# First feed-forward operands made ahead and kept in DRAM, and the step to the feed-forward without GpSimd arithmetic

## The chip, the cores and the metric

The kernel runs on one core of a Trainium2 chip. The metric is the device time of one execution in microseconds; a comparison takes the median of several executions. One execution was also recorded by the hardware profiler, and that one is read below.

## The reference

One encoder block on a sequence of 1024 tokens with 1024 channels, all float32. The part that matters here is the border between its two sub-layers:

```python
y = mixed @ w_out[l]
x = layer_norm(ALPHA * x + g1[:, None, :] * y, ln1_g[l], ln1_b[l])

h = modulate(layer_norm(x), sh2, sc2)
gt, up = jnp.split(h @ w_ffn_in[l], 2, axis=-1)          # 1024 x 2*2816
y = (jax.nn.silu(gt) * up) @ w_ffn_out[l]
x = layer_norm(ALPHA * x + g2[:, None, :] * y, ln2_g[l], ln2_b[l])
```

## The kernel before

**Number format.** Every float32 operand of a matrix product is kept as two float32r halves: `hi`, a cast on ScalarE, and `lo`, the difference source minus `hi`. The helper `split` (L96, L97) makes the pair, the difference on VectorE or on the engine it is given. A product is then three matmuls, hi·hi, hi·lo and lo·hi (`mm3`, L100 to L102).

**Stages.** Eight attention heads run one after the other, each in eight steps j; projections for the next head and other small jobs are put between the scores. Then come the eight token tiles of the output projection (`y0` to `y7`, 48 matmuls of 128x512 each), their residual, two layer norms and modulation, and a transpose by PE back to channels-by-tokens. Then the feed-forward runs over 22 column blocks f of 128, gate and up together, and its second matrix follows.

**The feed-forward as seven products.** Gate and up halves against the two token halves are multiplied by the Strassen-Winograd scheme: seven block products in place of eight. With token tiles 0 to 3 as the first half (`b11`, `b21`: upper and lower channels, in `h0h` and `h0l`) and tiles 4 to 7 as the second half (x12 and x22, in the raw tile `hr`), the activation side needs these operands, each with a hi and a lo:

- t1 = x12 − b11 (in `o1`), t2 = x22 − t1, in `oA`
- t3 = t2 − b11 in effect, also in `oA`; it is the same as x22 − x12
- b22 = x22 and t4 = b21 − t2, both in `oB`.

The weight side needs, for each f, the plain gate blocks (r11, r12: `first_w`, products `first_mm` into the PSUM tiles `fa` and `fb`), and five more operands: s1 = r21 + r22, s2 = s1 − r11, s3 = r11 − r21, s4 = r12 − s2 and r22 itself. For f = 0 the five are made by `rest_w` (L958 on) in six parts; for later f by the loop of the feed-forward. For f below 4 the plain products are made in the step itself and kept in the `p1` tiles.

**The step** is the stretch between the output projection and the feed-forward loop. It stands in a block with a manual schedule: on PE, VectorE, ScalarE and GpSimd the instructions stand exactly in the order in which they are written; each engine works its list in that order and waits at each instruction for what it needs. In the heads the order on each engine is made by a scheduler from priorities.

The short names of the step, with token tile t: `R` residual, `S1`/`A` statistics and affine of the first norm, `S2`/`N` the same of the second (`N`, L472, writes the normalised tile), `T` the transposes on PE, `M` the modulation on ScalarE (eight activations), `H` the split of tiles 0 to 3, `X` x12 − b11 (two subtractions, L1024 and L1025), `X2` t2 and `X2h`/`X2l` its halves, `X3` t3 and t4 in five parts, `B22h`/`B22l` the halves of b22, and `first_cp`/`first_add` the evacuation of a `first_mm`. `rstd` (L437, L93) are two tiny GpSimd instructions on which `A` and `N` wait. GpSimd also makes the lo of the four first weights (`wg_l`, 128x1024), the lo of b22, two of three steps of t3, one of t4 and two sums of `rest_w`.

At the end of f = 0 the products come in this order: a·t2, c·t1 (both in `rest_a`), a·t3, c·b22, a·t4, where a and c are the PSUM tiles `fa0` and `fc0`. ScalarE copies a (`u2`) and c (`p5`) after the first two, and VectorE adds a to `p5` (L1293) before a·t4 may write a again.

Of the kernel before, what the change touches and what calls it, by code (L numbers as in the profile page):

```python
# [35 lines left out]
def encoder_block_kernel(  # L36
# [445 lines left out]
    with ExitStack() as ctx2:  # L482
# [230 lines left out]


# [94 lines left out]
        for h in range(NH):  # L809
# [18 lines left out]
            else:  # L828
# [27 lines left out]
            for j in range(8):  # L856
# [56 lines left out]
    def first_w(f, rawg, eng=None):  # L913
# [44 lines left out]
    def rest_w(f, rawg, rawu, step):  # L958

        r11, r12, r21, r22 = rawg[:, 0:4, :], rawg[:, 4:8, :], rawu[:, 0:4, :], rawu[:, 4:8, :]  # L960
        if step == 0:
            ops_[f] = []
            ops_[f, "s"] = [evp.tile([P, 4, P], F32, tag="st", bufs=2, name="ws%d_%d" % (f, i)) for i in range(2)]

        def op_split(src):
            n = len(ops_[f])
            o = (fp.tile([P, 4, P], F32R, tag="oh", bufs=4, name="oh%d_%d" % (f, n)),
                 fp.tile([P, 4, P], F32R, tag="ol", bufs=4, name="ol%d_%d" % (f, n)))
            split(*o, src)
            ops_[f].append(o)  # L970

        sa, sb = ops_[f, "s"]
        if step == 0:
            pol(sa, r21, r22, op=ALU.add)
        elif step == 1:
            vec(sb, sa, r11, op=ALU.subtract)
            op_split(sb)
        elif step == 2:
            op_split(sa)
            pol(sa, r11, r21, op=ALU.subtract)  # L980
            vec(sb, r12, sb, op=ALU.subtract)
        elif step == 3:
            op_split(sa)
        elif step == 4:
            op_split(sb)
        else:
            op_split(r22)

    def X3(t, step):
        o11, o21 = [[o.bitcast(F32) for o in cut(b, t)] for b in (b11, b21)]  # L990
        x = hr[:, 4:8, tcol(t)]
        e = pol if t < 7 else vec
        if step == 0:
            f4_[t] = (ev_tile if t < 6 else th_tile)("h4s%d" % t).rearrange("p (a b) -> p a b", b=P)
            vec(f4_[t], o21[0], tt2[t], op=ALU.subtract)
        elif step == 1:
            e(x, tt2[t], o11[0], op=ALU.subtract)
            e(x, x, o11[1], op=ALU.subtract)
        elif step == 2:
            split(*cut(t3, t), x)  # L1000
        elif step == 3:
            pol(f4_[t], f4_[t], o21[1], op=ALU.add)
        else:
            split(*cut(t4, t), f4_[t])
# [60 lines left out]
    with tc.manual_schedule(engines={nc.vector.engine, nc.gpsimd.engine, nc.tensor.engine, nc.scalar.engine}):  # L1065
# [4 lines left out]
        R(5); S1(5); H(2); A(5); S2(5); N(5); H(3)  # L1070
        T(4); M(4)
# [20 lines left out]
        cps.close()
# [481 lines left out]
```

## Time and profile before

| | |
|---|---|
| median of 3 runs | 1627.44 us (1627.05 to 1629.0) |
| the profiled execution | 1627.82 us, span of its instructions 1626.0 us |
| mean granted TensorE clock | 0.986 |
| PE busy | 1564.6 us (96% of the span) |
| VectorE busy | 1170.9 us (72%) |
| ScalarE busy | 705.2 us (43%) |
| GpSimd busy | 359.1 us (22%) |

The span is read from the start of the first instruction. The heads end at about 845 us, the output projection runs to about 953 us, the step and f = 0 to about 1016 us, the feed-forward to about 1400 us. A busy PE is not a PE at its peak; what counts is where it is idle and at which clock it works.

### The profile page before, as it was taken

Reading aid. Unit: us, or ns where it says so; the run is one execution under the profiler, and the core shown is the slowest. Engines: PE = TensorE matmul, PEld = TensorE weight load, DVE = VectorE, ACT = ScalarE, POOL = GpSimd, SP = SyncE. Lnnn points to the kernel's source line nnn. Section 1 sums busy time; section 2 is a strip of 40 time slices with the busy share of each in tenths; the row PEclk is TensorE's granted clock in tenths of the full one; section 3 lists DMA queues with packets and bytes.
Section 4 is the critical chain, followed back from the end, with each engine's and each line's share of the span. In section 5 each row is a group of like instructions: output and inputs, shape, how many; then the busy total and the mean of one; then the engine's idle time right before and its main releaser. Section 6 shows DMA issues by size and latency. Waiting matters only on the chain. (4 is left out here: it accounts for less than half of the span.)

```text
span 1626.0 us, 20759 instructions
## 1 busy us (share of the span) xinstructions
PE 1564.6 (96%) x7634; PEld 1305.5 (80%) x7634; DVE 1170.9 (72%) x1690; ACT 705.2 (43%) x1224; POOL 359.1 (22%) x361
## 2 busy tenths in 40 slices
PE   5899999999999999999999986999999999999996
PEld 3787888888888888888878864888888888888885
DVE  7675868597775767576575799877877888436488
ACT  3445445454454545454471343444444444323220
POOL 4300001010001211100052255434333344100013
PEclk9999999999999999999999998999999999999999
DMA  9244415142332433221326631766666665996673
GB/s 333 59 114 143 139 62 147 59 136 88 109 102 71 150 110 92 78 52 47 91 97 203 192 117 38 240 229 211 233 233 223 230 227 182 349 398 228 201 269 133
DMA packets 187001, 260.79 MB, mean 160 GB/s; under 512 B 9682, under 2 KB 127507, under 8 KB 186899
## 3 DMA queue, kind: packets, MB, share of 16 engines
q1 hardware_dynamic: 181488, 244.75, 45.7%
q0 software_dynamic: 2448, 9.44, 1.5%
q10 hardware_dynamic: 2962, 5.27, 0.9%
q8 instruction: 60, 0.98, 0.2%
q14 instruction: 43, 0.34, 0.1%
HBM read 173.97 MB, written 77.07 MB: 154 GB/s over the span
## 5 line engine op out<-in xcount | busy, mean ns | idle before, releaser
L638 ACT ACTIVATE e<-e,nm 128x1024 f32<-128x1024 f32 x128 | 147.1, 1150 | 112.3 <-DVE nm L636 111.0
L636 DVE CUSTOM_DVE_ANT_0 e<-s,table 128x1024 f32<-128x1024 f32 x128 | 153.1, 1218 | 23.5 <-PE s L631 23.1
L97 DVE TENSOR_TENSOR al<-at,ah 128x512 fp32r<-128x512 f32 x128 | 83.2, 684 | 32.1 <-ACT ah L96 31.5
L629 PE MATMUL s<-k,q 128*128 128x512 f32 x256 | 105.2, 411 | 1.2 <-DVE nm L636 1.2
L631 PE MATMUL s<-k,q 128*128 128x512 f32 x256 | 101.5, 397 | 0.0
L96 ACT CAST oh<-ws 128x512 fp32r<-128x512 f32 x88 | 54.0, 616 | 85.7 <-POOL ws L1296 44.9
L97 DVE TENSOR_TENSOR ol<-ws,oh 128x512 fp32r<-128x512 f32 x88 | 73.5, 835 | 21.1 <-ACT oh L96 21.1
L643 DVE SCALAR_TENSOR_TENSOR e<-e,c,e 128x1024 f32<-128x1024 f32 x64 | 87.0, 1359 | 1.9
L97 DVE TENSOR_TENSOR fw<-fw,fw 128x512 fp32r<-128x512 f32 x77 | 82.1, 1066 | 0.2 <-ACT fw L96 0.2
L96 ACT CAST ah<-at 128x512 fp32r<-128x512 f32 x128 | 70.2, 597 | 27.7 <-PE at L652 27.6
L1296 POOL TENSOR_TENSOR ws<-rg,ru 128x512 f32<-128x512 f32 x21 | 44.3, 2110 | 148.3 <-DVE ol L97 140.7
L652 PE MATMUL at<-ident,e 128*128 128x128 f32 x512 | 69.8, 277 | 5.3 <-DVE e L643 3.2
L100 PE MATMUL av<-ah,vh 128*128 128x256 f32 x256 | 73.8, 288 | 0.3 <-ACT ah L96 0.2
L102 PE MATMUL av<-ah,vl 128*128 128x256 f32 x256 | 72.5, 283 | 0.0
L101 PE MATMUL av<-al,vh 128*128 128x256 f32 x256 | 72.4, 283 | 0.0
L100 PE MATMUL fa<-oA,oh 128*128 128x512 f32 x176 | 69.4, 395 | 2.7 <-ACT oh L96 2.7
L101 PE MATMUL fa<-oA,oh 128*128 128x512 f32 x176 | 69.4, 395 | 0.8 <-DVE oA L1052 0.8
L102 PE MATMUL oa<-w,mol 128*128 128x512 f32 x176 | 68.6, 390 | 1.2 <-DVE mol L97 1.2
L102 PE MATMUL fa<-oA,ol 128*128 128x512 f32 x176 | 69.3, 394 | 0.0
L100 PE MATMUL oa<-w,moh 128*128 128x512 f32 x176 | 68.6, 390 | 0.0
L101 PE MATMUL oa<-w,moh 128*128 128x512 f32 x176 | 68.5, 389 | 0.0
L652 PEld LDWEIGHTS at<-ident,e 128*128 128x128 f32 x512 | 59.4, 145 | 11.0 <-DVE e L643 3.6
(573 smaller groups left out, 4636.7 us busy)
## 6 DMA issues: line engine op xcount, KB each, us to landing
wfD<-fw SPq DMA_DIRECT2D x77, 512.0 KB, 3.4
w<-wfD SPq DMA_DIRECT2D x77, 512.0 KB, 4.8
ada<-in_w_ada_dram SPq DMA_DIRECT2D x32, 512.0 KB, 3.9
rg<-in_w_ffn_in_dram SPq DMA_DIRECT2D x26, 512.0 KB, 4.0
ru<-in_w_ffn_in_dram SPq DMA_DIRECT2D x22, 512.0 KB, 3.9
fw<-in_w_ffn_out_dram SPq DMA_DIRECT2D x44, 256.0 KB, 4.4
midD<-th SPq DMA_DIRECT2D x42, 256.0 KB, 2.2
q<-q SPq DMA_DIRECT2D x32, 256.0 KB, 2.9
```

The costliest lines, as they stand in the source:

```text
L96: nc.scalar.copy(hi, src)
L97: (eng or nc.vector).tensor_tensor(lo, src, hi.bitcast(F32), op=ALU.subtract)
L100: nc.tensor.matmul(ps, lh, rh, start=start, stop=False, skip_group_check=skip)
L101: nc.tensor.matmul(ps, lh, rl, start=False, stop=False, skip_group_check=skip)
L102: nc.tensor.matmul(ps, ll, rh, start=False, stop=stop, skip_group_check=skip)
L629: nc.tensor.matmul(ps[:, cs], q[:, 0, jj * P:(jj + 1) * P], kd[h, m][:, cs], start=True, stop=False)
L631: nc.tensor.matmul(ps[:, cs], q[:, 1, jj * P:(jj + 1) * P], kd[h, m][:, cs], start=False, stop=True)
L636: nc.vector.tensor_tensor_reduce(out=t, in0=ps, in1=table[:, o0:o0 + S], scale=-slope, scalar=3.0e38, op0=ALU.add, op1=ALU.min, accum_out=nm)
L638: nc.scalar.activation(t, t, AF.Exp, bias=nm, scale=-1.0, accum_out=zt[:, m, j:j + 1])
L643: nc.vector.scalar_tensor_tensor(s[1], s[1], c1, s[0], op0=ALU.mult, op1=ALU.add)
L652: nc.tensor.matmul(pt[:, i, :], a[:, kt * P:(kt + 1) * P], ident, start=True, stop=True, is_transpose=True)
L1296: pol(sa, blocks(n)[0], blocks(n)[2], op=ALU.subtract)
```

## The change

There are two parts.

**Weights ahead.** In heads 6 and 7 a generator, `ffn_units`, is called once for each step j from the second step of head 6 on. Each call makes one split of a 128x512 weight block into the tile `acc` (hi on ScalarE, lo on VectorE) and stores the pair to DRAM by SP's queue: eight units for the plain gate blocks of f = 1, 2, 3 and 0 (`wgD`), five for the operands of f = 0 (`opD`), thirteen in all, with four GpSimd additions in place and five loads of 512 KB. In the step, `first_w` and `first_op` load the finished halves by GpSimd's own DMA queue: eight loads of 512 KB and ten of 256 KB.

**The step.** `rest_w` is gone. t3 is now made as x22 − x12 (`D3`, `D3h`, `D3l`) before x12 is overwritten by `X`; the lo of b22 and both steps of t4 are on VectorE; the order of the parts is another. `early(1)`, the output tile 1, moves from the tail of head 7 to its last step.

```diff
+    wgD = dram.tile([4, 2, P, 2, HF], F32, tag="wgD", name="wgD")
+    opD = dram.tile([5, 2, P, HF], F32, tag="opD", name="opD")
...
+        def ffn_units():
...
+            def unit(dst, src, nm):
+                t = at.tile([P, 2, HF], F32R, tag="acc", name=nm)
+                split(t[:, 0, :], t[:, 1, :], src)
+                nc.sync.dma_start(dst.rearrange("a p c -> p a c"), t.bitcast(F32))
...
+            for f in (1, 2, 3):
+                yield from halves_of(f, gcols(f))
+            rg, ru = gcols(0), load_raw(wcols(wfi, DFF), "eu0")
+            yield from halves_of(0, rg)
+            r11, r12, r21, r22 = block(rg, 0), block(rg, 1), block(ru, 0), block(ru, 1)
+            unit(opD[4], r22, "ou4")
+            yield
+            pol(r22, r21, r22, op=ALU.add)
+            unit(opD[1], r22, "ou1")
...
-                    7: [lambda: rms_mix(h, 0, 1), lambda: early(0)],
+                    7: [lambda: rms_mix(h, 0, 1), lambda: early(0), lambda: early(1)],
...
+                elif h >= 6 and (h, j) > (6, 0):
+                    next(units, None)
...
-        split(*w, rawg, eng)
+        for a in range(2):
+            nc.gpsimd.dma_start(w[a].rearrange("p a b -> p (a b)").bitcast(F32),
+                                wgD[f, a].rearrange("p h c -> p (h c)"))
...
+    def first_op(n):
...
+        for a in range(2):
+            nc.gpsimd.dma_start(o[a].rearrange("p a b -> p (a b)").bitcast(F32), opD[n, a])
...
+    def D3(t):
+        d3_[t] = evp.tile([P, 4, P], F32, tag="st", bufs=2, name="d3_%d" % t)
+        vec(d3_[t], hr[:, 4:8, tcol(t)], hr[:, 0:4, tcol(t)], op=ALU.subtract)
...
+    def X3(t):
...
+        vec(f4_[t], o21[0], tt2[t], op=ALU.subtract)
+        vec(f4_[t], f4_[t], o21[1], op=ALU.add)
...
-        pol(o[1], hr[:, 4:8, tcol(t)], o[0].bitcast(F32), op=ALU.subtract)
+        vec(o[1], hr[:, 4:8, tcol(t)], o[0].bitcast(F32), op=ALU.subtract)
...
-        w_[0] = first_w(0, gload(0), nc.gpsimd)
         out_mm(6, mt[6], y_[6], (1,))
         T(5); M(5)
-        R(6); S1(6); X(4); A(6); S2(6); X(5); N(6)
-        w_[1] = first_w(1, gload(1), nc.gpsimd)
+        R(6); S1(6); D3(4); X(4); A(6); S2(6); D3(5); N(6); X(5)
+        w_[1] = first_w(1)
...
+        M(6); B22h(4); D3h(4); B22h(5); D3h(5)
+        R(7); S1(7); B22l(4); X2(4); A(7); S2(7)
         first_mm(0, w_[0])
         first_cp(0)
...
+        X2h(4)
         first_mm(1, w_[1])
+        first_add(0, False); N(7); T(7)
...
+        M(7)
+        w_[2] = first_w(2)
...
+        first_mm(2, w_[2])
+        w_[3] = first_w(3)
+        first_op(0)
+        D3(7); X(7); X2(7)
+        X2h(7); D3h(6); B22h(7); D3h(7)
+        first_cp(2)
...
+        X3s(4); X3(6); X3s(5); X3(7); X3s(6); X3s(7)
```

**Where the order moves.** GpSimd in the step, from the tiny `rstd` of token tile 7 on; before, with `wg_l` the lo of a first weight, `ws` a sum of `rest_w`, `oB` b22, `hr` t3:

```order
L437 TENSOR_SCALAR m_7rs<-m_7mv 128x1
L93 TENSOR_TENSOR m_7rs<-m_7rs,mhalf 128x1
L97 TENSOR_TENSOR wg_l<-rg_8456,wg_h 128x1024
L97 TENSOR_TENSOR wg_l<-rg_8503,wg_h 128x1024
L974 TENSOR_TENSOR ws_0_8543<-ru_8541 128x512
L1040 TENSOR_TENSOR oB<-hr,oB 128x4x128
L997 TENSOR_TENSOR hr<-hr,h0h 128x4x128
L998 TENSOR_TENSOR hr<-hr,h0l 128x4x128
L997 TENSOR_TENSOR hr<-hr,h0h 128x4x128
L998 TENSOR_TENSOR hr<-hr,h0l 128x4x128
L980 TENSOR_TENSOR ws_0_8543<-rg_8539,ru_8541 128x512
L997 TENSOR_TENSOR hr<-hr,h0h 128x4x128
```

and now, with `oh` and `ol` the halves of an operand of f = 0:

```order
L439 TENSOR_SCALAR m_7rs<-m_7mv 128x1
L95 TENSOR_TENSOR m_7rs<-m_7rs,mhalf 128x1
L964 DMA wg_h<-wgD 128x1024
L964 DMA wg_l<-wgD 128x1024
L964 DMA wg_h<-wgD 128x1024
L964 DMA wg_l<-wgD 128x1024
L973 DMA oh_0_8629<-opD 128x512
L973 DMA ol_0_8630<-opD 128x512
L973 DMA oh_1_8646<-opD 128x512
L973 DMA ol_1_8647<-opD 128x512
```

Arithmetic on GpSimd between these points is gone, and DMA issues stand there, behind the `rstd` of tile 7.

ScalarE at the end of f = 0, before; `p_3` is the copy of `fa3`, `u_0` and `p_0` the copies of a and c, `oB` the hi of t4, `th_0` the tanh of the gate, `oh` hi of weight operands:

```order
L929 COPY p_3_8654<-fa_8610 128x512
L1059 COPY u_0_8669<-fa_8415 128x512
L1062 COPY p_0_8683<-fc_8656 128x512
L96 CAST oh_3_8686<-ws_1_8544 128x512
L96 CAST oB<-h4s_8531 128x4x128
L96 CAST oB<-h4s_8533 128x4x128
L96 CAST oB<-h4s_8535 128x4x128
L96 CAST oB<-h4s_8648 128x4x128
L96 CAST oh_4_8698<-ru_8541 128x512
L1240 ACTIVATE th_0_8712<-p_0_8441 128x512
```

and now:

```order
L986 COPY p_3_8692<-fa_8663 128x512
L1090 COPY u_0_8717<-fa_8492 128x512
L1093 COPY p_0_8731<-fc_8704 128x512
L98 CAST oB<-h4s_8698 128x4x128
L98 CAST oB<-h4s_8701 128x4x128
L98 CAST oB<-h4s_8736 128x4x128
L1268 ACTIVATE th_0_8762<-p_0_8518 128x512
L98 CAST oB<-h4s_8741 128x4x128
L98 CAST oh_0_8768<-ws_1_8756 128x512
```

The copies of a and c still stand ahead of the hi of t4; what stood between and behind them for the weights of f = 0 is gone.

VectorE from the add for f = 3 to the add of a to `p5`, before (the last row is the add; `h4s` is t4 before its split):

```order
L934 TENSOR_TENSOR p_3_8654<-p_3_8654,fb_8611 128x512
L97 TENSOR_TENSOR ol_3_8687<-ws_1_8544,oh_3_8686 128x512
L97 TENSOR_TENSOR oB<-h4s_8531,oB 128x4x128
L97 TENSOR_TENSOR oB<-h4s_8533,oB 128x4x128
L97 TENSOR_TENSOR oB<-h4s_8535,oB 128x4x128
L97 TENSOR_TENSOR oB<-h4s_8648,oB 128x4x128
L97 TENSOR_TENSOR ol_4_8699<-ru_8541,oh_4_8698 128x512
L1245 SCALAR_TENSOR_TENSOR th_0_8712<-th_0_8712,p_0_8441 128x512
L1276 TENSOR_TENSOR ws_1_8710<-ws_0_8709,rg_8705 128x512
L97 TENSOR_TENSOR ol_0_8719<-ws_1_8710,oh_0_8718 128x512
L1288 TENSOR_TENSOR ws_1_8710<-rg_8705,ws_1_8710 128x512
L1293 TENSOR_TENSOR p_0_8683<-p_0_8683,fa_8415 128x512
```

and now:

```order
L991 TENSOR_TENSOR p_3_8692<-p_3_8692,fb_8664 128x512
L99 TENSOR_TENSOR oB<-h4s_8698,oB 128x4x128
L1031 TENSOR_TENSOR h4s_8736<-h0h,hr 128x512
L1032 TENSOR_TENSOR h4s_8736<-h4s_8736,h0l 128x512
L99 TENSOR_TENSOR oB<-h4s_8701,oB 128x4x128
L1031 TENSOR_TENSOR h4s_8741<-h0h,t2s 128x512
L1273 SCALAR_TENSOR_TENSOR th_0_8762<-th_0_8762,p_0_8518 128x512
L1032 TENSOR_TENSOR h4s_8741<-h4s_8741,h0l 128x512
L99 TENSOR_TENSOR oB<-h4s_8736,oB 128x4x128
L1306 TENSOR_TENSOR ws_1_8756<-ws_0_8755,rg_8751 128x512
L99 TENSOR_TENSOR oB<-h4s_8741,oB 128x4x128
L99 TENSOR_TENSOR ol_0_8769<-ws_1_8756,oh_0_8768 128x512
L1318 TENSOR_TENSOR ws_1_8756<-rg_8751,ws_1_8756 128x512
L1323 TENSOR_TENSOR p_0_8731<-p_0_8731,fa_8492 128x512
```

The two steps of t4 for tiles 6 and 7 now stand between the lo of the tiles before them.

## Rows read from the trace of the kernel before

**Rows 1.** Busy time by stretch: the last head but one, then the step in three pieces.

```profile
core 0: us, PE busy (x) PEld busy (x) DVE busy (x) ACT busy (x) POOL busy (x), PEclk, DMA share, GB/s
640.00:740.00 100.00, 99.84 (x533) 85.28 (x532) 68.15 (x108) 49.98 (x88) 8.68 (x19) 1.00 0.23 72
935.00:960.00 25.00, 21.46 (x103) 17.43 (x102) 22.74 (x26) 11.74 (x29) 12.17 (x11) 1.00 0.38 123
960.00:985.00 25.00, 19.95 (x89) 15.35 (x87) 23.76 (x21) 8.71 (x17) 19.44 (x13) 1.00 0.21 67
985.00:1016.00 31.00, 20.48 (x59) 15.42 (x60) 28.36 (x34) 13.68 (x26) 14.65 (x9) 0.75 0.16 47
```

**Rows 2.** PE in order of time: where it waited in the step, and two speeds.

```profile
start us, us, engine line op out<-in xcount [idle before <-releaser]
941.48 1.06 PE L458 MATMUL m_5t<-ident,m_5n 128*128 128x128 f32 x8 [1.65 <-DVE m_5n L472]
955.35 1.06 PE L458 MATMUL m_6t<-ident,m_6n 128*128 128x128 f32 x8 [1.89 <-DVE m_6n L472]
...
957.65 0.39 PE L100 MATMUL fa<-h0h,wg_h 128*128 128x512 f32 x1
957.88 0.39 PE L101 MATMUL fa<-h0l,wg_h 128*128 128x512 f32 x1
...
969.13 1.09 PE L458 MATMUL m_7t<-ident,m_7n 128*128 128x128 f32 x8 [1.80 <-DVE p L934]
...
995.20 0.77 PE L100 MATMUL fc<-o,oh 128*128 128x512 f32 x1 [4.24 <-DVE p L934]
...
1011.36 0.76 PE L100 MATMUL fa<-oB,oh 128*128 128x512 f32 x1 [5.20 <-DVE p L1293]
1011.92 0.63 PE L101 MATMUL fa<-oB,oh 128*128 128x512 f32 x1
1012.35 0.63 PE L102 MATMUL fa<-oB,ol 128*128 128x512 f32 x1
```

**Rows 3.** VectorE in order of time, the same columns as Rows 2.

```profile
904.51 0.81 DVE L472 TENSOR_SCALAR z<-z,m_2mv,m_2rs 128x1024 f32<-128x1024 f32 x1 [1.19 <-DMA x1D<-z]
...
938.48 2.85 DVE L472 TENSOR_SCALAR m_5n<-zx,m_5mv,m_5rs 128x1024 f32<-128x1024 f32 x1 [1.00 <-POOL m_5rs L93]
...
985.84 0.69 DVE L1052 TENSOR_TENSOR oA<-t2s,oA 128x512 fp32r<-128x512 f32 x1
986.44 0.69 DVE L97 TENSOR_TENSOR ol<-ws,oh 128x512 fp32r<-128x512 f32 x1
...
987.64 6.81 DVE L97 TENSOR_TENSOR o<-hr,o 128x512 fp32r<-128x512 f32 x4
...
1010.53 0.68 DVE L1293 TENSOR_TENSOR p<-p,fa 128x512 f32<-128x512 f32 x1
```

**Rows 4.** GpSimd in order of time, the same columns.

```profile
938.41 2.37 POOL L97 TENSOR_TENSOR wg_l<-rg,wg_h 128x1024 fp32r<-128x1024 f32 x1
...
964.70 0.87 POOL L93 TENSOR_TENSOR m_7rs<-m_7rs,mhalf 128x1 f32<-128x1 f32 x1
...
988.84 1.73 POOL L997 TENSOR_TENSOR hr<-hr,h0h 128x512 f32<-128x512 f32 x1
```

**Rows 5.** Waits of PE in heads 0 to 3, 160 to 560 us: all there are.

```profile
engine line waited for: us in total, times, longest us
PE at L652 <- DVE vl L97: 0.4, 2, 0.3
```

**Rows 6.** DMA issues: line, size, median us from issue to landing.

```profile
rg<-in_w_ffn_in_dram SPq DMA_DIRECT2D x26, 512.0 KB, 4.0
...
mA<-midD POOLq DMA_DIRECT2D x1, 1024.0 KB, 8.0
...
midD<-th POOLq DMA_DIRECT2D x2, 256.0 KB, 5.8
```

**Rows 7.** VectorE and GpSimd in order of time, beside a software DMA.

```profile
1401.37 1.29 DVE L97 TENSOR_TENSOR m_ol<-raw_m,m_oh 128x512 fp32r<-128x512 f32 x2
...
1401.76 0.84 POOL L1234 DMA_DIRECT2D midD<-th  x1 [20.96 <-DVE th L1233]
```

**Rows 8.** ScalarE in order of time: modulation of one token tile, the copy of c.

```profile
956.02 2.90 ACT L463 ACTIVATE hr<-m_6t,modc 128x128 f32<-128x128 f32 x8 [1.53 <-PE m_6t L458]
...
1000.67 0.59 ACT L1062 COPY p<-fc 128x512 f32<-128x512 f32 x1 [0.70 <-PE fc L102]
```

More of the change, by code (lines that the diff above doesn't have):

```diff
@@ L712, in mix, with block, gcols, halves_of @@
             nc.sync.dma_start(mixD[:, h * P:(h + 1) * P, cs].rearrange("a p s -> p a s"), mh.bitcast(F32))
+        def ffn_units():
+            nxt = {}
+            def block(r, i):
+                return r[:, 4 * i:4 * i + 4, :].rearrange("p a b -> p (a b)")
+            def unit(dst, src, nm):
+                t = at.tile([P, 2, HF], F32R, tag="acc", name=nm)
+                split(t[:, 0, :], t[:, 1, :], src)
+                nc.sync.dma_start(dst.rearrange("a p c -> p a c"), t.bitcast(F32))
+            def gcols(f):
+                return load_raw(wcols(wfi, f * P), "eg%d" % f)
+            def halves_of(f, r):
+                for i in range(2):
+                    unit(wgD[f, :, :, i, :], block(r, i), "wu%d_%d" % (f, i))
+                    yield
[5 more added lines that the diff above has]
+            unit(opD[4], r22, "ou4")
+            yield
+            pol(r22, r21, r22, op=ALU.add)
+            unit(opD[1], r22, "ou1")
+            yield
+            pol(r21, r11, r21, op=ALU.subtract)
+            unit(opD[2], r21, "ou2")
+            yield
+            pol(r11, r22, r11, op=ALU.subtract)
+            unit(opD[0], r11, "ou0")
+            yield
+            pol(r12, r12, r11, op=ALU.subtract)
+            unit(opD[3], r12, "ou3")
+            yield
+        units = ffn_units()
         ada_jobs = [(j, k) for j in (2, 4, 3, 5) for k in range(KT)]
@@ L836, in encoder_block_kernel @@
                     6: [lambda: wo_prep(4), lambda: wo_prep(5), lambda: wo_prep(6), lambda: wo_prep(7)],
-                    7: [lambda: rms_mix(h, 0, 1), lambda: early(0)],
+                    7: [lambda: rms_mix(h, 0, 1), lambda: early(0), lambda: early(1)],
                 }
-                tail_fill = [lambda: early_load(2), lambda: early_load(3), lambda: early(1),
+                tail_fill = [lambda: early_load(2), lambda: early_load(3),
                              lambda: early_load(4), lambda: ln_rows(),
@@ L956, in encoder_block_kernel @@
     ops_ = {}
[L958 to L1004, printed above, removed]
+    d3_ = {}
@@ new lines, in D3, with D3h, D3l @@
+    def D3(t):
+        d3_[t] = evp.tile([P, 4, P], F32, tag="st", bufs=2, name="d3_%d" % t)
+        vec(d3_[t], hr[:, 4:8, tcol(t)], hr[:, 0:4, tcol(t)], op=ALU.subtract)
+    def D3h(t):
+        nc.scalar.copy(cut(t3, t)[0], d3_[t])
+    def D3l(t):
+        o = cut(t3, t)
+        vec(o[1], d3_[t], o[0].bitcast(F32), op=ALU.subtract)
+    def X3(t):
+        o21 = [o.bitcast(F32) for o in cut(b21, t)]
+        f4_[t] = (ev_tile if t < 6 else th_tile)("h4s%d" % t).rearrange("p (a b) -> p a b", b=P)
+        vec(f4_[t], o21[0], tt2[t], op=ALU.subtract)
+        vec(f4_[t], f4_[t], o21[1], op=ALU.add)
@@ L1006, in encoder_block_kernel, with X3s @@
+    def X3s(t):
+        split(*cut(t4, t), f4_[t])
     f4_ = {}
@@ L1079, in encoder_block_kernel @@
         T(6)
-        B22h(4); B22h(5); M(6); B22l(4)
-        R(7); S1(7); X2(4); X2h(4); B22h(6); B22l(5); B22l(6)
+        M(6); B22h(4); D3h(4); B22h(5); D3h(5)
+        R(7); S1(7); B22l(4); X2(4); A(7); S2(7)
         first_mm(0, w_[0])
         first_cp(0)
-        A(7); S2(7); X2(5); X2l(4)
-        w_[2] = first_w(2, gload(2), nc.gpsimd)
+        X2h(4)
         first_mm(1, w_[1])
+        first_add(0, False); N(7); T(7)
         first_cp(1)
+        B22h(6)
+        first_add(1, False)
+        B22l(5); X2(5); D3l(4); D3(6); B22l(6); X(6); X2(6)
         X2h(5)
-        N(7); first_add(0, False); T(7)
-        w_[3] = first_w(3, gload(3), nc.gpsimd)
         M(7)
+        w_[2] = first_w(2)
         cps.close()
@@ L1258, in encoder_block_kernel @@
                 pol(sa, blocks(n)[2], blocks(n)[3], op=ALU.add)
+            if f == 0:
+                first_op(4)
             if f >= BR:
```

32 lines of the change are left out of this document (12 added, 20 removed).

## The prediction

> **What bounds the kernel now.** I read the busy time by stretch first. In the heads PE is busy 99.84 of 100 us while VectorE has 32 us free and ScalarE 50 [rows 1], so PE is the bound there. In the step it is not: from 935 to 1016 us PE idles 3.5, 5.1 and 10.5 us in the three stretches, 19.1 us together, VectorE is busy 75 of the 81 us, and in the last stretch PE's granted clock is 0.75 [rows 1]. The chain that ended last, on the profile's page, covers only the last 64 us of the kernel and says nothing of the step, so I went on to PE in order of time. Almost every wait there ends on VectorE: on `N` before the transposes of tiles 5 and 6, on `N` of tile 7 (the releaser named is its neighbour), on an add before c·t1, and on the add to `p5` before a·t4 [rows 2].
>
> Why is VectorE late? The same instruction `N` takes 0.81 us at 904.51 and 2.85 us at 938.48 [rows 3]; at 938.41 GpSimd has just begun a `wg_l` of 2.37 us [rows 4]. Free two-input instructions of 512 columns start 0.60 us apart, but the four lo of t1 at 987.64 take 6.81 us in place of 2.4 [rows 3], beside GpSimd's t3 [rows 4]. VectorE thus stands still while GpSimd computes, and GpSimd is busy 19.4 of the 25 us from 960 on [rows 1]. The four lo of t1 and the three `N` alone (2.0 each) lose 10.5 us to it.
>
> The waits cost PE twice. Its products of 512 columns start 0.23 us apart at 957 us, and 0.43 us apart after the wait of 5.20 us [rows 2]: the lower of the two levels, 1.2 GHz in place of 2.4. Twelve such products lose 2.4 us. After waits of 1.65 and 1.89 us the clock stayed at 1.00 [rows 1, 2].
>
> **The step, part by part.** I walk it in the times of the profiled execution. A two-input VectorE instruction counts 0.60 per 512 columns [rows 3]; a cast on ScalarE about 0.6, by the copy of 0.59 [rows 8].
>
> *Tiles 5 and 6.* `N` of tile 5 still starts at 938.48, but without `wg_l` it takes 0.8; both waits, 1.65 and 1.89, go [rows 2]. The transposes of tile 6 come at 955.35 − 3.5 = 951.8. One `D3` (0.6) is new ahead of `N` of tile 6; VectorE's own gain of 2 us covers it.
>
> *Tile 7.* PE then has 0.8 us of transposes and 48 products of 0.2275 us (10.9): it is free at 963.5. VectorE from 951.8: residual and statistics 2.6; then the lo of b22 waits for ScalarE, which puts the modulation of 2.90 us [rows 8] ahead of the cast (0.7 to its start, 2.9, 0.6: 956.0, a wait of 1.6); b22 and t2 1.2, affine 2.4, statistics 1.4, and 1.0 for the `rstd`, as before tile 5 [rows 3]: `N` starts at 962.0 and ends at 962.8. The transposes come at 963.5 in place of 969.13 [rows 2], 5.6 earlier, PE the later by 0.7. What is late next is a transfer.
>
> *The weights of f = 2.* Their two loads stand on GpSimd's queue behind the `rstd` of tile 7, so they issue at 962.0 and, 0.84 us later [rows 7], 962.8, although their buffers are free from 958 on. Behind them wait the loads of f = 3 and of the operands, needed later. The trace has no 512 KB load of this queue. The nearest: 4.0 us on SP's queue, and on GpSimd's own 5.8 us for 256 KB and 8.0 us for 1 MB [rows 6]. I take 5.0, nearer to SP's row of the same size, since GpSimd's rows lie where the DMA engines were full; both ends stay for the range. PE, free at 964.3, begins the third pair at about 967.3: a new wait of 3.0 us, with some 2 us of low clock behind it (between 1.89, where none came, and 4.24).
>
> The Trainium skill, "DMA: Bandwidth & Descriptors", section "Anatomy of one DMA — SWDGE (gpsimd) path", puts such a transfer at 2.0 us plus the bytes at 436 GB/s. By it 512 KB would take an estimated 3.2 us; but for 256 KB it says 2.6 where the row has 5.8.
>
> *PE to the end of f = 0.* Pairs 2 and 3: 10.9 + 2.0, to 980.2. a·t2 (12 products, 2.7) to 982.9, c·t1 to 985.7, a·t3 and c·b22 to 991.1. The operands of f = 0 issue from 964.5 to 971 and land by 976: nothing.
>
> *VectorE to the end of f = 0.* From 963.5, an add and twelve instructions, to 971.3; `D3`, `X` and t2 of tile 7, to 973.7; now ScalarE must do six casts and copies before t1's first lo can follow (3.1): 976.9. Thirteen instructions, 7.8, and one GpSimd sum (`ws`) that holds VectorE about 1.1: at 985.8 it reaches the lo of t4. ScalarE has the copy of c ahead of that cast: 985.7 + 0.6 + 0.6 = 986.9. Twelve instructions more, 7.2, and 0.3 of waits for single casts: the add to `p5` starts at 994.4. PE followed it by 0.83 before (1010.53 to 1011.36) [rows 2, 3], so a·t4 comes at 995.2. It has waited 4.1 us and runs at the low clock, as before. Shift: 1011.36 − 995.2 = **16.2 us**. From there both run the same list with PE as the bound.
>
> Three VectorE instructions more than before (twelve come: four `D3`, four lo of b22, four of t4; nine go: two sums, five lo of weights, two of t3) are in these counts.
>
> **The heads.** Thirteen splits (0.6 on each of ScalarE and VectorE), four GpSimd additions, five loads and thirteen stores are new in a stretch where VectorE is free 32 us in 100. Fully exposed on both engines they would cost 15.6 us; nothing is the other end, and a gain is excluded since PE has no idle time to give. The nearest row: in heads 0 to 3 each of 32 steps carries one VectorE instruction of twice that width, and PE's waits there are 0.4 us in 400 [rows 5]. I take 0.5, and nothing for moving `early(1)`: PE's list is only re-sorted, and what is delayed, the last attention block, is wanted at the end of y4, with y2 and y3 (2 × 10.9 us) in between.
>
> **Sum.** 16.2 − 0.5 = 15.7. The profiled execution took 1627.82, so 1612.1; it lies 0.4 above the median of the runs. Forecast **1612 us**, 1610 to 1615 as this case's own range.
>
> **Rivals.**
>
> *The transfers come sooner.* At 4.0 us or less the wait at pair 2 is under 2 us, the clock stays up, and VectorE alone sets the end: 985.8 + 7.5 + 0.8 = 994.1; without the hold by `ws`, 993. Gain 17 to 18, and 2 more if the last wait also keeps the clock: 1607 to 1610. For it: SP's row. Against it: 5.8 us for half the size.
>
> *They come later.* At 8.0 us everything from pair 2 on moves by 3.0: gain 12.7, 1615. At 10 or more the weights of f = 1 (issued at 951, wanted at 958) hold PE too, and with it tile 7: gain about 8, 1619. A DMA issue itself does not hold VectorE: two lo beside one took 1.29 us, 0.6 each [rows 7]. The Trainium skill, "SBUF — State Buffer", section "SBUF: two separate sides", says that GpSimd cannot write its descriptors while VectorE runs an instruction that uses both port pairs. `N` of tile 7 starts just where the loads of f = 2 issue; that would add up to 0.8 us, and no row here shows it.
>
> *It does not do what it says.* If VectorE's long instructions were not GpSimd's doing, VectorE would have three more and nothing else: plus 1.8, 1629. The pair 0.81 and 2.85 speaks against it.
>
> *Slower, by SP's queue in the heads.* Each store waits for its lo, and SP's list holds the weight loads and q copies of the next head behind it. A projection that comes so late that PE waits 4.24 us costs, with the low clock, 6.6. From three such waits on the change loses; four give 1612 + 26 = 1638. Against it: the 32 us in 100 that VectorE has free.
>
> **Chances.** Forecast 0.55, sooner 0.20, later 0.17, no effect 0.04, heads 0.04. For 8 in 10: 1606 to 1619, which leaves out no effect, the heads and the far ends of sooner and later. This kernel's runs tell 0.2% (3.3 us) from no change: faster 0.91, same 0.05, slower 0.04.
>
> **What would show it.** `N` of tiles 5 to 7 near 0.8 us and t1's four lo near 2.4; no wait before the transposes of tiles 5, 6 and 7; a wait of 2 to 4 us before the third pair that ends on a DMA; a·t4 at 993 to 997, again behind the add to `p5`; PE busy over 99 of 100 us in heads 6 and 7. It is wrong if PE waits in the heads, if VectorE stays slow beside DMA issues, or if the weights of f = 1 land after 958.

## The result, and the profile after

| | before | after |
|---|---|---|
| median | 1627.94 us (1627.05 to 1629.0, 4 runs) | 1616.71 us (1615.88 to 1617.57, 4 runs) |
| ratio | | 0.9931, 95% interval 0.9914 to 0.9948 |
| profiled execution, span | 1627.82, 1626.0 us | 1616.56, 1614.8 us |
| mean granted clock | 0.986 | 0.991 |

The change is faster by 11.2 us. The forecast was 15.7 us, 1612.1 in the profiled execution. The time lies 4.5 us above that: outside the forecast's own range of 1610 to 1615, and inside the range of 8 in 10, 1606 to 1619. The busy time by stretch, of the kernel after, in the stretches of [rows 1]:

```profile
core 0: us, PE busy (x) PEld busy (x) DVE busy (x) ACT busy (x) POOL busy (x), PEclk, DMA share, GB/s
640.00:740.00 100.00, 99.85 (x534) 85.32 (x533) 71.22 (x114) 52.77 (x94) 9.13 (x19) 1.00 0.38 119
935.00:960.00 25.00, 24.59 (x121) 20.12 (x120) 22.01 (x31) 10.64 (x28) 10.12 (x14) 1.00 0.51 185
960.00:985.00 25.00, 22.41 (x100) 17.69 (x99) 21.00 (x33) 12.14 (x26) 7.71 (x15) 1.00 0.51 191
985.00:1016.00 31.00, 24.93 (x102) 20.14 (x101) 25.27 (x37) 11.41 (x20) 9.35 (x8) 0.89 0.39 127
```

Head 6 carries the new splits (VectorE 3.1 us more, ScalarE 2.8) and PE is as busy as before, 99.85 of 100; in head 7, from 740 to 845 us, it is busy 104.28 of 105 us, before 104.29. The heads cost nothing. From 935 to 1016 us PE's idle time falls from 19.1 to 9.1 us. PE of the kernel after in order of time, its waits (in brackets the idle time before the row and what released it):

```profile
start us, us, engine line op out<-in xcount [idle before <-releaser]
850.45 1.09 PE L654 MATMUL at<-ident,e 128*128 128x128 f32 x8 [3.19 <-DVE e L645]
858.75 0.50 PE L102 MATMUL y<-wo_h,mx_0h 128*128 128x512 f32 x1 [2.42 <-ACT mx_0h L98]
896.57 1.07 PE L460 MATMUL m_0t<-ident,z 128*128 128x128 f32 x8 [0.45 <-DVE z L474]
907.03 1.06 PE L460 MATMUL m_1t<-ident,z 128*128 128x128 f32 x8 [0.53 <-DVE z L474]
942.39 1.07 PE L460 MATMUL m_5t<-ident,m_5n 128*128 128x128 f32 x8 [0.26 <-DVE m_5n L474]
969.53 0.47 PE L102 MATMUL fa<-h0h,wg_h 128*128 128x512 f32 x1 [2.02 <-DMA wg_h<-wgD]
970.73 0.50 PE L104 MATMUL fa<-h0h,wg_l 128*128 128x512 f32 x1 [0.50 <-DMA wg_l<-wgD]
998.75 0.76 PE L102 MATMUL fa<-oB,oh 128*128 128x512 f32 x1 [6.07 <-issue]
999.31 0.63 PE L103 MATMUL fa<-oB,oh 128*128 128x512 f32 x1
999.74 0.63 PE L104 MATMUL fa<-oB,ol 128*128 128x512 f32 x1
1395.30 0.50 PE L102 MATMUL ob<-w,moh 128*128 128x512 f32 x1 [1.58 <-ACT moh L98]
```

Of the waits before the transposes of tiles 5 to 7 only 0.26 us is left, at tile 5, and the 4.24 us before c·t1 [rows 2] are gone. So are two before a·t2 in the kernel before:

```profile
985.25 0.49 PE L100 MATMUL fa<-oA,oh 128*128 128x512 f32 x1 [2.69 <-ACT oh L96]
986.58 0.61 PE L101 MATMUL fa<-oA,oh 128*128 128x512 f32 x1 [0.83 <-DVE oA L1052]
```

In their place stand 2.52 us for the weights of f = 2, and a·t4 still waits, 6.07 us, with low clock behind it (rows 0.43 apart from 999.31 on). It starts 12.6 us earlier than in [rows 2]. VectorE of the kernel after, the rows that answer to [rows 3]:

```profile
941.43 0.81 DVE L474 TENSOR_SCALAR m_5n<-zx,m_5mv,m_5rs 128x1024 f32<-128x1024 f32 x1 [1.00 <-POOL m_5rs L95]
953.55 0.81 DVE L474 TENSOR_SCALAR m_6n<-zx,m_6mv,m_6rs 128x1024 f32<-128x1024 f32 x1 [0.77 <-POOL m_6rs L95]
965.54 0.81 DVE L474 TENSOR_SCALAR m_7n<-zx,m_7mv,m_7rs 128x1024 f32<-128x1024 f32 x1 [0.44 <-POOL m_7rs L95]
981.04 2.50 DVE L99 TENSOR_TENSOR o<-hr,o 128x512 fp32r<-128x512 f32 x4 [1.87 <-ACT o L98]
985.25 1.79 DVE L1071 TENSOR_TENSOR oB<-hr,oB 128x512 fp32r<-128x512 f32 x1
997.97 0.68 DVE L1323 TENSOR_TENSOR p<-p,fa 128x512 f32<-128x512 f32 x1
```

All three `N` take 0.81 us, t1's four lo 2.50, and one lo of b22 is held for 1.1 by the GpSimd sum `ws`. `N` of tile 5 starts 2.95 us later than before, and from there to the add to `p5` it is 56.5 us; the prediction said 55.9. The profile names no releaser for a·t4 ("issue"); it starts 0.78 us behind that add, in the kernel before 0.83.

Two losses lie outside the step: those 2.95 us ahead of it, and the wait of 1.58 us at 1395, which the kernel before does not have.

### The profile page after: what moved, and what is told of

It is laid out like the page before. It is cut to its first block, busy times and chain, and to the rows that moved or that the text cites. A ratio compares the mean times of both kernels' runs of the same rounds, so it can differ in the third digit from the quotient of the medians.

```text
span 1614.8 us, 20838 instructions
## 1 busy us (share of the span) xinstructions
PE 1558.5 (97%) x7634; PEld 1299.6 (80%) x7634; DVE 1161.7 (72%) x1706; ACT 706.2 (44%) x1228; POOL 338.4 (21%) x363
## 5 line engine op out<-in xcount | busy, mean ns | idle before, releaser
L654 PEld LDWEIGHTS at<-ident,e 128*128 128x128 f32 x512 | 58.8, 144 | 11.2 <-DVE e L645 3.6
```

The costliest lines, as they stand in the source:

```text
L654: nc.tensor.matmul(pt[:, i, :], a[:, kt * P:(kt + 1) * P], ident, start=True, stop=True, is_transpose=True)
```

## Experiments

Times are medians; ratios are to the kernel before on the same chip, with their 95% intervals. An edit is to the kernel after unless it says "before".

**early(1) at its old place, and early(1) moved alone.**

```diff
-  7: [..., lambda: early(0), lambda: early(1)],
+  7: [..., lambda: early(0)],
-  tail_fill = [lambda: early_load(2), lambda: early_load(3),
+  tail_fill = [lambda: early_load(2), lambda: early_load(3), lambda: early(1),
```

> The changed kernel with the start of the last attention block, early(1), back at its old place behind the eight steps of head 7; all else as changed. Theory: moving early(1) puts six products of y1 ahead of the last product of y0 and takes the transposes of the last block out of the place where they filled PE, so that PE waits 2.42 us at mx_0h and then runs eight products at the low clock; that is the about 3 us by which N of tile 5 starts later (941.43 against 938.48). With it back: no wait at mx_0h, N of tile 5 near 938.5, a·t4 near 995.8, median 1613.7 (1612.5 to 1615). Rival: the thirteen units in heads 6 and 7 or the transfers they bring delay the end of the heads; then N of tile 5 stays at 941 and the time within 0.7 us of the changed kernel's 1616.7.

> The kernel before with early(1) alone moved into the last step of head 7. Theory: the same re-sorting of PE's list, a wait of about 2.4 us at mx_0h, and since everything behind it follows N of tile 5, about 3 us slower: 1630.9 (1629.5 to 1632). Rival (the units do the delay): no change, 1627.9, no wait at mx_0h over 1 us.

Measured: back 1615.13 us, 0.9916 [0.9903, 0.993]; moved alone (before) 1629.67, 1.0008 [0.9999, 1.0017], 1.3 us slower with an interval that just takes in no change. The second time lies in the theory's range and the first 0.1 us outside it, but the time alone does not show a price. The traces of both directions agree on one thing: with early(1) moved PE waits about 0.5 us before the transposes of tile 0 and of tile 1, with the old place it does not. But my account of the wait at `mx_0h` fell. It was absent in the second profile of the kernel after and in the one with early(1) moved alone, and it stood at 1.8 us in kernels with early(1) at the old place. It goes with something else: of five executions whose transposes behind the 3.2 us wait at 850 ran at full clock (1.09 us, granted clock 1.00) four have it, and none of the nine where they ran at the low one (1.97 us, 0.50). PE of the kernel with early(1) back:

```profile
851.83 1.97 PE L654 MATMUL at<-ident,e 128*128 128x128 f32 x8 [3.19 <-DVE e L645]
...
996.91 0.76 PE L102 MATMUL fa<-oB,oh 128*128 128x512 f32 x1 [6.08 <-issue]
997.47 0.63 PE L103 MATMUL fa<-oB,oh 128*128 128x512 f32 x1
```

Counted from that transpose row (851.02 in before, 850.45 in after), and so free of what happens earlier, PE reaches these points (us; the products are the first of each kind in PE's rows):

| | tile 5's transposes | a·t4 | f = 1 | f = 2 | f = 4 |
|---|---|---|---|---|---|
| before | 90.5 | 160.3 | 165.6 | 179.6 | 207.4 |
| after | 91.9 | 148.3 | 153.0 | 166.6 | 194.3 |
| after, a second profile | 90.6 | 146.8 | 152.0 | 166.0 | 194.4 |
| early(1) back | 88.7 | 145.1 | 149.9 | 163.5 | 191.3 |
| before, weights ahead alone | 88.7 | 147.6 | 150.3 | 163.9 | 191.6 |
| the same, a second profile | 89.4 | 148.2 | 150.9 | 164.5 | 192.6 |
| before, arithmetic on VectorE alone | 90.1 | 158.2 | 162.6 | 176.2 | 204.0 |
| old addresses | 89.7 | 145.9 | 150.2 | 163.8 | 191.6 |
| VectorE's list shorter | 88.8 | 141.0 | 144.2 | 165.4 | 192.7 |
| copy of c ahead, first version | 88.5 | 140.5 | 143.8 | 158.8 | 188.5 |
| the same, second version | 89.4 | 141.8 | 145.0 | 162.9 | 190.6 |

Two profiles of one kernel differ by up to 1.5 us in this table, so smaller differences between kernels show nothing by themselves.

**The two parts of the change, each alone, on the kernel before.**

```diff
+ the units in heads 6 and 7, first_w and first_op as DMA (weights ahead alone)
```
```diff
-  pol(o[1], hr[:, 4:8, tcol(t)], ...)        # B22l
+  vec(o[1], hr[:, 4:8, tcol(t)], ...)
-  e = pol if t < 7 else vec                  # t3
+  e = vec
-  pol(f4_[t], f4_[t], o21[1], op=ALU.add)    # t4
+  vec(f4_[t], f4_[t], o21[1], op=ALU.add)
```

> The kernel before with only the first part: weight operands of f = 0 to 3 made in heads 6 and 7 and loaded by the software queue; the step's order, and the arithmetic on GpSimd of t3, t4 and the lo of b22, stay as before; early(1) stays. Theory (GpSimd's arithmetic holds VectorE's two-input instructions): N of tiles 5 to 7 takes 0.8 us, the three waits before T5 to T7 go (5.3 us), t1's four lo still take over 5 us beside t3 on GpSimd, and the last wait shrinks by the five lo and two sums of weights that VectorE no longer makes (4.2 us): gain 7 to 10, 1618 to 1621. Rival (the order is what helps): gain under 4 us, 1624 to 1628.

> The kernel before with only the arithmetic of the step moved: lo of b22, both steps of t3 and the second step of t4 on VectorE in place of GpSimd, in the old order; the first weights are still split in the step, their lo on GpSimd. VectorE gets 16 instructions more of about 0.6 us, 9.6 us. Theory (a GpSimd instruction holds VectorE for most of its length): the sixteen GpSimd instructions of about 1.6 us cost VectorE at least as much as it now does itself; t1's four lo come down to 2.4 us; N of tiles 5 and 7 stays near 2.8 us beside wg_l; time within -6 and +1 us of before: 1622 to 1629. Rival (VectorE is simply short of time): its list is 9.6 us longer up to the add to p5 and a·t4 comes that much later: 1635 to 1638.

Measured: weights ahead alone 1613.74, 0.9911 [0.9896, 0.9926], 14.6 us faster, more than either the theory or the rival gave and no less than the whole change; arithmetic on VectorE alone 1625.62, 0.9984 [0.9975, 0.9992], 2.7 us, inside the range of its theory. (The second edit moves fourteen instructions, six of t3, four lo of b22 and four of t4, and not the sixteen of the expectation.) VectorE of the kernel with the weights ahead alone:

```profile
976.15 6.85 DVE L99 TENSOR_TENSOR o<-hr,o 128x512 fp32r<-128x512 f32 x4
...
983.52 4.30 DVE L1055 TENSOR_TENSOR hr<-t2s,h0h 128x512 f32<-128x512 f32 x1
...
997.73 0.68 DVE L1349 TENSOR_TENSOR p<-p,fa 128x512 f32<-128x512 f32 x1
```

its GpSimd beside the second of these rows:

```profile
983.50 3.77 POOL L1060 TENSOR_TENSOR h4s<-h4s,h0l 128x512 f32<-128x512 f32 x3
```

and its PE:

```profile
990.23 0.79 PE L102 MATMUL fa<-oA,oh 128*128 128x512 f32 x1 [3.53 <-ACT u L1117]
...
995.96 0.47 PE L102 MATMUL fc<-oB,oh 128*128 128x512 f32 x1 [1.02 <-DMA oh<-opD]
...
998.90 0.39 PE L102 MATMUL fa<-oB,oh 128*128 128x512 f32 x1
999.13 0.39 PE L103 MATMUL fa<-oB,oh 128*128 128x512 f32 x1
```

GpSimd still holds VectorE there: t1's four lo take 6.85 us, and one instruction of t3 takes 4.30 in place of 0.69. Yet the add to `p5` comes 58.6 us behind `N` of tile 5 (939.1), against 56.5 in the kernel after. Between these two points VectorE has 51 instructions of 512 columns there and 61 in the kernel after. The ten fewer, 6.0 us at 0.6 each, pay for most of the 8.1 us that it loses more to holds and waits (6.0 + 58.6 − 56.5). And what is left of the lead, the clock takes: here PE waits in pieces and a·t4 runs at 0.23 us a product; with the new order it waits 6.1 us in one piece and runs nine products at 0.43. At f = 1 the weights ahead alone and the new order (early(1) back) lie 0.4 us apart (150.3 and 149.9 in the table), at f = 4 0.3, less than the 1.0 between the two profiles of the weights ahead alone.

In the kernel with the arithmetic moved alone, the weights' lo on GpSimd still hold `N`, so the waits before tiles 5 and 7 stay; t1's lo come down as they should. Its VectorE and its PE:

```profile
938.56 2.84 DVE L472 TENSOR_SCALAR m_5n<-zx,m_5mv,m_5rs 128x1024 f32<-128x1024 f32 x1 [1.00 <-POOL m_5rs L93]
...
990.40 2.49 DVE L97 TENSOR_TENSOR o<-hr,o 128x512 fp32r<-128x512 f32 x4
```

```profile
941.54 1.88 PE L458 MATMUL m_5t<-ident,m_5n 128*128 128x128 f32 x8 [2.02 <-DVE m_5n L472]
970.81 1.09 PE L458 MATMUL m_7t<-ident,m_7n 128*128 128x128 f32 x8 [3.38 <-DVE p L934]
1009.67 0.57 PE L100 MATMUL fa<-oB,oh 128*128 128x512 f32 x1 [4.50 <-DVE p L1293]
```

**The load of f = 2 ahead of the rstd of tile 7** (with early(1) back).

```diff
-  R(7); S1(7); B22l(4); X2(4); A(7); S2(7)
-  first_mm(0, w_[0])
+  R(7); S1(7); B22l(4); X2(4); A(7)
+  first_mm(0, w_[0])
+  w_[2] = first_w(2)
+  S2(7)
```

> The changed kernel with early(1) back, and the loads of the weights of f = 2 issued on GpSimd's queue ahead of the rstd of tile 7 instead of behind it, so that they land before PE wants them. Theory (VectorE's list sets the end of f = 0, as the prediction said): the waits of 1.97 and 0.56 us before the third pair go, the last wait, before a·t4, grows by as much, from 6.08 to 8.3-8.7 us, a·t4 stays at the same distance from N of tile 5 (57.3 us), and the time stays within 0.7 us of the kernel with early(1) back alone (1615.13). Rival (PE and its transfers set the end): a·t4 comes 2.5 us earlier and the time falls to 1612.6 or below.

Measured: 1615.75, 0.9926 [0.9915, 0.9938]. PE of this kernel:

```profile
982.46 0.47 PE L102 MATMUL fc<-o,oh 128*128 128x512 f32 x1 [2.23 <-ACT u L1090]
...
996.97 0.76 PE L102 MATMUL fa<-oB,oh 128*128 128x512 f32 x1 [6.07 <-issue]
```

The 2.53 us for the transfer are gone, a wait of 2.23 stands at c·t1 instead, and a·t4 comes at 996.97 against 996.91 with early(1) back alone. VectorE sets the end of f = 0, as predicted; only the place of the new wait was another than expected.

**VectorE's list shorter** (with early(1) back), and both edits together.

```diff
+  D3l(6); B22l(7); D3l(7)
   for t in range(4, 8): split(*cut(t1, t), ...)
...
-  D3l(6); D3l(7); B22l(7)
...
   # f = 0: X3s(6); add to p5; X3s(7); then the operands of f = 1,
   # the gate's product and first_add(3), which stood ahead of the add
```

> The changed kernel with early(1) back, and VectorE's list in the step in another order, nothing added or removed: the last two lo of t3 and the last of b22 stand ahead of the lo of t1, where VectorE waited 1.87 us for ScalarE; the add to p5 stands ahead of the last lo of t4; and five instructions that a·t4 doesn't need (sum of the fourth pair, the gate's product, three on the operands of f = 1) stand behind it. Theory (VectorE sets the end): the add comes 4.5 to 6 us earlier, a·t4 waits under 2 us and keeps the high clock (12 products, 2.4 us more): 1608 to 1611. Rival (the wait is only moved): the operands of f = 1 come late instead, PE waits there for 4 us or more, 1613.5 to 1616.

> Both edits together: the loads of f = 2 ahead of the rstd, and VectorE's shorter list. Theory: VectorE still sets the end, so the loads give nothing more: within 1 us of the kernel with the shorter list alone, 1607 to 1611, with a wait of 2 to 4 us before a·t4. Rival: with VectorE short, PE's own list is the bound, and the 2.5 us of the transfer are gained on top: 1606 to 1608.

Measured: 1615.98, 0.9926 [0.9915, 0.9938], and 1616.98, 0.9930 [0.9919, 0.9942]. The theory of the shorter list was right on a·t4 and wrong on the time, which is the rival's: the wait is moved. Both edits together are no faster, as their theory said, but miss the time that it gave; PE waits 0.56 us at a·t4 and 4.45 one block later. PE of the kernel with the shorter list, and below it its ScalarE, then its VectorE:

```profile
992.83 0.47 PE L102 MATMUL fa<-oB,oh 128*128 128x512 f32 x1 [0.99 <-ACT oB L98]
...
1008.76 0.80 PE L102 MATMUL fc<-oB,oh 128*128 128x512 f32 x1 [4.41 <-ACT p L1314]
```

```profile
1006.12 0.62 ACT L98 CAST oh<-ws 128x512 fp32r<-128x512 f32 x1 [4.90 <-DVE ws L1306]
1007.61 0.62 ACT L98 CAST fw<-fw 128x512 fp32r<-128x512 f32 x1 [0.87 <-DMA fw<-in_w_ffn_out_dram]
1008.13 0.58 ACT L1314 COPY p<-fc 128x512 f32<-128x512 f32 x1
```

```profile
999.90 0.68 DVE L991 TENSOR_TENSOR p<-p,fb 128x512 f32<-128x512 f32 x1
...
1005.34 0.68 DVE L1306 TENSOR_TENSOR ws<-ws,rg 128x512 f32<-128x512 f32 x1
```

a·t4 comes 4.1 us earlier and keeps its clock; all of it is lost one block later, where c·b22 of f = 1 waits 4.41 us for ScalarE's copy of c. That copy stands behind two casts. The first, of an operand of f = 2, waits 4.90 us for VectorE's sum `ws`; the second, of the second matrix, waits 0.87 us for a transfer. VectorE works from 998.69 to that sum without a gap, and the sum of the fourth pair (999.90) and the gate's product, which the edit put behind the add, are in this stretch. So what the shorter list put off came due one block later.

The copy comes at nearly the same time with early(1) back, 1008.19, and with the weights ahead alone, 1008.28, and I took it for a gate that the step does not move. ScalarE with early(1) back says otherwise:

```profile
1007.14 0.62 ACT L98 CAST oh<-ws 128x512 fp32r<-128x512 f32 x1 [1.60 <-PE fc L103]
1007.67 0.61 ACT L98 CAST fw<-fw 128x512 fp32r<-128x512 f32 x1
1008.19 0.58 ACT L1314 COPY p<-fc 128x512 f32<-128x512 f32 x1
```

Here the first cast waits for PE itself, the second for no transfer, and the copy keeps up with PE. The equal times have different causes; in the kernel after the copy comes at 1009.92, and with the old addresses, below, at 1005.86.

**The kernel after once more.**

> The changed kernel once more, for its difference to the others on one chip and for one question: is the wait of 1.58 us at 1395.30, on ScalarE's first cast behind the feed-forward, which the kernel before has not, there again? If the order of the step or the place of the end sets it: 1.5 to 2.0 us again, 1616.7. If the transfers fall by chance: none in this profile, and a profiled execution near 1615.

Measured: 1615.25, 0.9924 [0.9912, 0.9936], span 1615.0. The wait at 1395 is there again (1.4 us), as in all kernels so far with the new step (1.3 to 2.3), and in none with the old one.

**The addresses.** In the kernel after, ScalarE's first cast behind the feed-forward, and the GpSimd store of `th` ahead of it:

```profile
1394.63 3.75 ACT L98 CAST moh<-m 128x512 fp32r<-128x512 f32 x7 [7.27 <-issue]
```

```profile
1388.08 0.56 POOL L1262 DMA_DIRECT2D midD<-th  x1 [20.94 <-DVE th L1261]
```

The profile names no releaser, but the slower of the two stores takes 6.5 us to land, and 1388.08 + 6.5 = 1394.6, where the cast begins. The same sum meets the cast within 0.1 us in all six profiles that have the wait. In the compiled program ScalarE waits ahead of this cast for the semaphore of that store, and the cast's tile, `moh` 2, and the `th` that this store reads stand at the same address, 188256; in the kernel before that `th` stands at 180064. The pool of the step gives addresses by which tag is asked for first: before, the sources of t4 (`ev`, `th`); after, the operands that now come by DMA (`oh`, `ol`). The experiment only asks for the old ones first:

```diff
   th_tile = lambda nm: fp.tile(...)
+  for t in (4, 5, 6):
+      f4_[t] = (ev_tile if t < 6 else th_tile)("h4s%d" % t)...
```

> The changed kernel with one thing different: three tiles of the step (the sources of t4) are allocated a few lines earlier, ahead of the first operand tile; no instruction is added, moved or removed. This puts the four tags of the pool at the addresses that they have in the kernel before. Theory: the wait of 1.3 to 2.3 us at 1395, in every kernel with the new step and in none with the old one, is that of the first cast behind the feed-forward for the last store of th by the software queue, because its tile lies over that th; with the old addresses it lies elsewhere and the wait goes: 1.3 to 2.0 us faster than the changed kernel, 1613.3 to 1614.8. Rival (the feed-forward's end comes sooner than the transfer of m that the cast reads): the wait stays, 1615.3 to 1616.7.

Measured: 1613.06, 0.9906 [0.9892, 0.9919]; no wait at 1395. ScalarE of this kernel:

```profile
1386.81 2.71 ACT L98 CAST moh<-m 128x512 fp32r<-128x512 f32 x5 [3.46 <-PE ob L103]
```

The cast waits for a product as in the old kernels and PE does not wait for it. From the first product of the second matrix to the transposes behind its first block PE takes 14.24 us, in the kernel after 16.36 and before 14.22, so the wait and the slow restart behind it cost 2.1. The gain over the kernel after, about 2.9 to 4 us by the ratios, is more than that, and the time is 0.2 us below the theory's range; the intervals allow the 2.1.

**The copy of c ahead of the casts.** The shorter list, early(1) back, the old addresses, and in f = 1 the copy of c ahead of the two casts; in the first version the step of the second matrix's preparation was left out in f = 1, in the second it stands behind the copy. The cut is against the kernel with the shorter list.

```diff
-  if more and f > 0: vec(sb, ...); operand(n, sb)
+  if more and f > 1: vec(sb, ...); operand(n, sb)
...
-  if f > 0: fw_step()
+  if f > 1: fw_step()
   ...                # c·t1 and the copy p5
+  if f == 1: vec(sb, ...); operand(n, sb)      # second version: fw_step() too
```

> The kernel with early(1) back and VectorE's shorter list, with the addresses of the kernel before, and in f = 1 alone ScalarE's copy of c (p5) ahead of two casts that stood in front of it: the first operand of f = 2, and the first operand of the feed-forward's second matrix, whose DMA lands at 1007.6 whatever the step does. Theory: that copy, at 1008.1 to 1008.3 in all of these kernels, is the next gate, so what PE gains before a·t4 was lost at c·b22 of f = 1 (4.41 us and the low clock after it); without it PE runs through: no wait over 2 us between 970 and 1100, 2 us fewer at 1395: 1607 to 1610. Rival (the operands of f = 2 come late in their turn, VectorE being the bound through f = 1 too): 1612 to 1614, with a wait of over 3 us in f = 1 or f = 2.

> The last kernel (VectorE's shorter list, early(1) back, addresses of the kernel before, the copy of c in f = 1 ahead of two casts), but the step of the second matrix's preparation that was left out in f = 1 stands behind that copy instead, so that the preparation keeps its pace through the feed-forward. Theory: the 4.21 us at 1391.83, for a transfer of the second matrix queued on SP behind stores that came late, were the price of the step left out; without it, 1610 to 1612.5. Rival (the transfers are the bound from 1375 on, DMA share 1.0 there in every kernel, so that a PE which comes sooner waits for them anyway): a wait of 2 us or more behind 1375 again, 1613 to 1615.

Measured: 1615.59, 0.9923 [0.9909, 0.9936], and 1611.66, 0.9903 [0.989, 0.9917]. PE of the first version, and of the second:

```profile
1391.83 0.76 PE L102 MATMUL ob<-w,moh 128*128 128x512 f32 x1 [4.21 <-DMA w<-wfD]
```

```profile
991.65 0.47 PE L102 MATMUL fa<-oB,oh 128*128 128x512 f32 x1 [0.99 <-ACT oB L98]
...
1008.34 0.50 PE L102 MATMUL fa<-oB,oh 128*128 128x512 f32 x1 [2.38 <-DVE p L1332]
```

The first version was 3.1 us ahead of the kernel with the old addresses at f = 4 (188.5 against 191.6 from the transpose row) and gave it back for one transfer, so its time is outside both ranges on record for it. Keeping the pace of the preparation took that wait away and brought 3.3 us by the ratios, inside the theory's range. The second version has the lowest ratio of the study, but it too pays in f = 1: it enters f = 1 5.2 us ahead of the old addresses and leaves it 0.9 ahead, by 2.38 us at a·t4 and the low clock behind it. That wait is again for an add at the end of VectorE's list (L1332): as the rival of the first version said, VectorE is the bound through f = 1 too. The lead over the simpler kernel with the old addresses is within the intervals.

**Weights ahead alone, again.**

> The kernel before with the weights ahead alone, once more, on the same chip as the last candidate. Question: is the new order of the step worth anything, once its addresses cost nothing? The changed kernel with the old addresses ran at 0.9906 [0.9892, 0.9919] of before. Theory (nothing: sixteen more instructions on VectorE cost what GpSimd's hold gives back): 0.990 to 0.992 again, 1612.5 to 1615. Rival (worth 3 us or more, 1613.74 was luck): 0.9925 to 0.994, 1616 to 1618.

Measured: 1612.75, 0.9915 [0.9901, 0.9928], inside the theory's range. The changed kernel with the old addresses is 0.8 and 1.5 us ahead of the two runs by the ratios. That is inside the intervals, and early(1) at its new place, 1.3 us [−0.2, +2.8], is still in that kernel and not in these; so the new order may be worth some 2 to 3 us, and these runs do not tell it from nothing.

## Why the prediction was right, and where its terms were off

- *Tiles 5 to 7: right.* `N` 0.81 three times, the three waits gone, 0.26 us left at tile 5.
- *Weights of f = 2: right in kind, half in price.* 3.0 us and 2 of low clock were predicted; measured 2.02 + 0.50 and no drop. The two loads issue at 965.47 and 966.48 and land 3.9 and 4.2 us later, which is SP's row and not the 5.0 taken between the rows [rows 6]; the two for f = 3, issued right behind them, take 6.3 and 7.0. The Trainium skill, "DMA: Bandwidth & Descriptors", section "Anatomy of one DMA — SWDGE (gpsimd) path", gives an estimated 3.2 us for this size; the trace does not agree, 3.9. The first issue took 1.01 us beside `N` of tile 7 and 0.61 where no `N` ran beside it (the load ahead of the rstd): 0.4 us of issue, while `N` itself took 0.81 as always. The rule of the Trainium skill, "SBUF — State Buffer", section "SBUF: two separate sides", that GpSimd cannot write descriptors while VectorE runs an instruction on both port pairs, would give up to 0.8 if `N` is such an instruction; the trace agrees in kind, with 0.4.
- *VectorE sets the end of f = 0: right, and shown* by the load ahead, which moved nothing. From `N` of tile 5 to a·t4 57.3 us in place of 72.9: 15.6 against the 16.2 predicted. t1 waited for ScalarE 1.87 us in place of 3.1; the predicted wait of t4's lo for ScalarE did not come.
- *The last wait: mis-sized.* 4.1 us predicted, 6.07 measured, since the transfer cost PE 2.5 instead of 5.0. It cost nothing more, because VectorE set the end. The clock behind it was not "as before": nine rows 0.43 apart follow, before fourteen, which gives back 1.0 us.
- *"Nothing for moving early(1)": the step that failed.* The step starts 2.95 us later. About 1.0 are the waits at tiles 0 and 1, shown by undoing and by doing it alone; at a·t4 in the table the pairs whose transposes at 850 ran at the same clock lie 1.7 (after again, early(1) back) and 1.85 (moved alone, before) apart. The rest of the 2.95 goes with that clock and the wait at `mx_0h`, which come and go between executions of one program; what sets them is not shown. In the time, early(1)'s price is 1.3 us [−0.2, +2.8], which takes in none.
- *"From there both run the same list": failed, 2.1 us.* The list is the same, the addresses were not, and a cast 400 us later waited for a store.
- *The reason given for VectorE: right row by row, wrong as the price of the second part.* GpSimd does hold it (6.85 and 2.50 for the same four lo). But the sum set the hold that goes and the twelve instructions that come in one walk, and I did not price the first part by itself. That part alone gives 14.6 and 14.9 us by the medians (0.9911 and 0.9915); with equal addresses the whole change has 0.9906, so what the new order and VectorE's arithmetic add cannot be told from nothing.

Sum of the profile after: 12.6 us at a·t4; 13.7 at f = 4 (1058.44 − 1044.78), with the shorter low clock; less 2.1 at 1395, 11.5 behind the second matrix's first block, and 11.2 between the spans. The loss ahead of the step, 2.95, and the one at 1395 make the forecast too high; that the clock gave 1.0 back was luck.

## What to carry to other kernels

Price each part of a change alone before pricing the sum: here one part alone gave as much as the whole (14.6 against 11.2 us, and 0.9911 against 0.9906 once the addresses were equal). Whether the gains of the two parts add (14.6 and 2.7 alone) these runs do not tell, since the whole also carries early(1). Behind a wait that goes, look for what the instructions that were put off will hold up next, here VectorE's own list one block later. That an event comes at the same time in several kernels does not make it a fixed gate: look in each at what released it. And where tiles are allocated in another order, look at which tiles share an address: a cast may wait for a store that has nothing to do with it.

## What was not expected of the hardware

After one and the same wait of 3.2 us at 850, the eight transposes took 1.97 us at a granted clock of 0.50 in some executions and 1.09 at 1.00 in others of the same program (the kernel after: 1.09, then 1.97; weights ahead alone: 1.97, then 1.09). One two-input VectorE instruction of 512 columns took 4.30 us beside a run of GpSimd additions, six times its 0.69 (weights ahead alone, at 983.52). Eight software DMA issues in a row, 0.54 us each, left VectorE's instructions beside them 0.6 to 0.7 us apart (the kernel after, from 966.48 us on).
